# Grouping a scan's small products and moving rotary work to VectorE in an encoder trunk on one Trainium2 core

## The chip, the cores and the metric

The kernel runs on one core of one Trainium2 chip. A core has TensorE (PE in the rows; its weight loads are PEld), VectorE (DVE), ScalarE (ACT), GpSimd (POOL) and SyncE (SP), each with a program of its own that it works off in order, and semaphores between them. The metric is the device time of one execution in microseconds; less is better. The time of a kernel is the median of its runs.

## The reference

The kernel computes a trunk of two post-norm layers on one sequence of 512 tokens, width 1024. Each layer has three groups of heads (differential attention with partial rotary embedding, a bidirectional gated linear recurrence, cross-attention into 256 memory tokens), one output projection, a layer norm, a gated MLP of width 2816 with a width-3 convolution, and a layer norm. Everything is float32. Cut to what matters here:

```python
def hybrid_layer(x, mem, cos, sin, layer, w_in, ...):
    da_q, da_k, da_v, hg_q, hg_ff, hg_fb, hg_i, hg_g, mx_q = jnp.split(x @ w_in, split_idx, axis=-1)
    dq = rope_partial(da_q.reshape(B, S, DA_HEADS, 2, DA_HEAD_DIM), cos, sin) * (DA_HEAD_DIM ** -0.5)
    dk = rope_partial(da_k.reshape(B, S, DA_HEADS, 2, DA_HEAD_DIM), cos, sin)
    ...                                   # differential softmax attention -> da_o
    o_fwd = hgrn2_chunk_scan(hq, -jnp.expm1(g_f), hv, g_f)
    o_bwd = jnp.flip(hgrn2_chunk_scan(...reversed in time...), 1)
    ...                                   # gate and norm -> hg_o; memory attention -> mx_o
    mix = jnp.concatenate([da_o, hg_o, mx_o], axis=-1) @ w_out
    x = layer_norm(DEEPNORM_ALPHA * x + mix, ln1_g, ln1_b)
    u = depthwise_conv_centred(x @ w_up, conv_w, conv_b)
    gate, val = jnp.split(u, 2, axis=-1)
    return layer_norm(DEEPNORM_ALPHA * x + (jax.nn.silu(gate) * val) @ w_down, ln2_g, ln2_b)

def rope_partial(t, cos, sin):            # the first 16 of 64 columns are rotated
    t1, t2 = t[..., :half], t[..., half:ROPE_DIM]
    return jnp.concatenate([t1 * cos - t2 * sin, t2 * cos + t1 * sin, t[..., ROPE_DIM:]], axis=-1)
```

## The kernel before, in words

**Products.** Every large float32 product is made of three float16 products: each operand is split into a high and a low part, and high·high, high·low and low·high are added in PSUM. A weight is read, scaled by a power of two from its sum of squares, and split by `prep`: ScalarE makes the high part, VectorE the low part (L311, `wl`). The same is done for activations (`xh` and `xl`; behind a layer norm, ScalarE at L292 and VectorE at L293 from transposed tiles `tr`) and for the input of the out projection (`mgh`, `mgl`; L545, L547).

**The scan.** Two heads form a unit, two units a layer, so there are four scans. `hg_attn` computes the recurrence by doubling block lengths m = 1, 2, 4 to 256: at each level TensorE makes small products of blocks of both directions for each of the two heads, ScalarE (for small blocks also VectorE at L851 and GpSimd at L854) puts them into a matrix, and VectorE multiplies the decays of a level into Q (L881, on a tile called `t` in the rows), into K (L885) and into the table of decays (L888). The products of the low levels have 32 output partitions, those of m = 64 have 64, the last ones 128. In the rows these are `sc<-t,w 128*32`, `sc<-t,t 128*64` and so on; large products are 128*128. Differential attention contracts over 64 rows (64*128).

**Rotary.** `rope_step` makes a tile of the q or k projection: TensorE's 24 products of 512 columns, then VectorE shuffles the columns (L1003), GpSimd multiplies by the sine (L1004), VectorE multiplies by the cosine (L1005) and adds (L1006), ScalarE rounds to the high part (L1008) and GpSimd subtracts for the low part (L1009). There are 16 such tiles.

**Out projection and LN1.** The out projection is done in parts as groups of heads finish (`down_part`): a product group into a PSUM bank `mm`, which VectorE then adds to the residual `z` (L569). There are two banks for `mm`, three for `sc`, two for `tr` and one for `stat`. When a token tile of `z` is complete, it is normalised (L227 to L232, then L280 and L281 on VectorE, in halves of 512 columns), transposed on TensorE (L288), and split into `xh` and `xl` for the up-projection. LN1 is this layer norm, once in each layer.

**The order.** The program is recorded once, through generators that take turns by credits (a `yield` with a number gives up a turn of that cost; `HG_COST` is 1.6 in the scan). A planner then orders each engine's instructions: it takes the recorded operations with costs (`cost_of`) and the buffers that they hold, simulates the engines, and picks on each engine, among the operations that are ready, the one with the earliest due time. On ScalarE a change of the function table is charged. TensorE's 64-row products take their buffers in runs of six. Which instruction stands where on an engine is thus an outcome of the plan, not of the code's order.

Of the kernel before, what the change touches and what calls it, by code (L numbers as in the profile page):

```python
# [95 lines left out]
def trunk(ctx: ExitStack, tc: tile.TileContext, a, out, slots=None):  # L96
# [595 lines left out]
    def build_layer(l):  # L692
# [55 lines left out]
        def hg_units(pr):  # L748
# [57 lines left out]
            def hg_attn():  # L806
                mix = new_mix(("hg", pr))
                Qs, Ks, As, Ds, Ts = [], [], [], [], []
                for j in range(2):
                    f, q = hs["f", j], hs["q", j]  # L810
                    Q = tmp([P, 2, 512], "t4", bufs=4)
                    K = tmp([P, 2, 512], "t4", bufs=4)
                    V.tensor_tensor(Q, f, q.unsqueeze(1).broadcast_to([P, 2, 512]), ALU.mult)
                    for d in range(2):
                        V.tensor_scalar(K[:, d, :], f[:, 1 - d, :], -1.0, 1.0, ALU.mult, ALU.add)
                    ks = tmp([P, 512], "w2", bufs=4)
                    V.tensor_tensor(ks, K[:, 0, :], K[:, 1, :], ALU.add)
                    At = tmp([P, 4, 512], "t8", bufs=2)
                    Dg = tmp([P, 4, 32], "hgD", bufs=2)
                    p_ = psc()  # L820
                    for c in range(4):
                        for b in range(4):
                            cs = slice(c * P + 32 * b, c * P + 32 * b + 32)
                            mm(p_[32 * b : 32 * b + 32, c * 32 : c * 32 + 32], ks[:, cs], q[:, cs], True, True)
                    A.activation(Dg, p_[:, 0:P].rearrange("p (c t) -> p c t", c=4), AF.Identity)
                    Qs.append(Q)
                    Ks.append(K)
                    As.append(At)
                    Ds.append(Dg)
                    Ts.append(f)  # L830
                    yield HG_COST

                def diag_block(At, s0, t0, n):
                    v = At[s0 : s0 + n, 0, :]
# [3 lines left out]
                while m < S:  # L838
                    nb = S // m
                    for j in range(2):  # L840
# [37 lines left out]
                        if m < 256:  # L878
# [7 lines left out]
                            if m < 128:  # L886
                                Tn = tmp([P, 2, nb // 2], f"hgT{j}_{m.bit_length() % 2}")
                                V.tensor_tensor(Tn, tv[:, :, :, 0], tv[:, :, :, 1], ALU.mult)  # L888
                                Ts[j] = Tn
                        yield HG_COST  # L890
                    m *= 2
                while ("g", 1) not in hs or "v" not in hs:
                    yield None
# [99 lines left out]
        def da_units(pr):  # L993
            ds_ = {}

            def rope_step(ws, key):
                iv = inv_of(ws[0], qin[:, l : l + 1], 0.125 if key == "q" else 1.0)
                ds_["i" + key] = iv
                for j in range(2):
                    p_ = pmm()  # L1000
                    gemm_f(p_, ws[0], j * P, xact)
                    q = tmp([P, 512], "sg", bufs=2)
                    V.stream_shuffle(q, p_, SHUF)  # L1003
                    G.tensor_tensor(q, q, ropes, ALU.mult)  # L1004
                    V.tensor_tensor(p_, p_, ropec, ALU.mult)  # L1005
                    V.tensor_tensor(q, q, p_, ALU.add)  # L1006
                    hl = tmp([P, 2, 512], "qg", F16, bufs=NQG)
                    A.activation(hl[:, 0, :], q, AF.Identity)  # L1008
                    G.tensor_tensor(hl[:, 1, :], q, hl[:, 0, :], ALU.subtract)  # L1009
                    ds_[key, j] = hl  # L1010
                    yield
                if key == "k":
                    ds_["iqk"] = small(1, "iqk", bufs=2)
                    V.tensor_tensor(ds_["iqk"], ds_["iq"], ds_["ik"], ALU.mult)
# [207 lines left out]


class Op:
    __slots__ = ("i", "name", "eng", "cost", "tail", "reads", "writes", "table", "preds", "succs", "tiles", "dmab", "line", "kind", "small", "order_ins", "mv", "istr", "half")


def cost_of(i, kind, eng, outs, ins):
# [56 lines left out]
def extract(instrs):  # L1285
    ops = []
    last_half = None
    for i in instrs:
# [32 lines left out]
        if o.eng == "PE":  # L1321
            if "float16" in str(ins[0].dtype) and ins[0].ap[0][1] == 64:
                o.half = ins[0].offset // ins[0].ap[0][0]
                if last_half not in (None, o.half):
                    o.cost, last_half = 0.005, None
                else:
                    last_half = o.half
            else:
                last_half = None
        ops.append(o)  # L1330

    cache = {}
# [28 lines left out]
    for o in ops:  # L1361
# [16 lines left out]
        for wr, bs in ((False, o.reads), (True, o.writes)):  # L1378
            for b in bs:
# [6 lines left out]
                    else:  # L1386
                        h[:] = [e for e in h if not (p0 <= e[2] and e[3] <= p1 and (e[4] & ~m) == 0 and e[0] != o.i)]
                h.append((o.i, wr, p0, p1, m))
    for o in ops:
        for p in o.preds:  # L1390
            ops[p].succs.append(o.i)
    for o in [o for o in ops if o.dmab][:FIRST]:
        o.dmab *= FAST
    run = []
    for o in ops + [None]:
        if o is not None and o.eng != "PE":
            continue
        if o is not None and o.half is not None:
            run.append(o)
            continue  # L1400
        for k in range(0, len(run), 6):
            both = list(dict.fromkeys(t for p in run[k : k + 6] for t in p.tiles))
            for p in run[k : k + 6]:
                p.tiles = both
        run = []
    return ops, tiles


def simulate(ops, tiles, prio, fixed=None, wait=0.0, log=None):
# [5 lines left out]
    end = [0.0] * N  # L1415
    free = {e: 0.0 for e in ("PE", "DVE", "ACT", "POOL", "SP")}
    table = 0
    dma_free = 0.0

    users = defaultdict(list)  # L1420
# [54 lines left out]
    while done < N:  # L1475
# [24 lines left out]
        if i is None:  # L1500
            a = avail[e]
            lim = t + wait
            i = min((x for x in a if ready[x] <= t + 1e-9), key=lambda x: (prio[x] + (PEN if e == "ACT" and ops[x].table and ops[x].table != table else 0), x))
            if wait:
                w = min((x for x in a if ready[x] <= lim), key=lambda x: prio[x])
                if prio[w] < prio[i]:
# [11 lines left out]
        if e == "ACT" and o.table and o.table != table:  # L1518
            c += 1.28
            table = o.table  # L1520
        start[i] = t
        if o.dmab:
            free[e] = t + o.cost
# [28 lines left out]

PEN = 20.0
SHARE = 0.35
FIRST = 9
FAST = 205 / 370.0

# [88 lines left out]
```

## Time and profile before

| | us |
|---|---|
| median of 3 runs (1499.23 to 1501.7) | 1501.5 |
| profiled execution | 1502.42 |
| its span | 1500.6 |
| TensorE busy | 1457.2 (97%) |
| VectorE busy | 1153.8 (77%) |
| ScalarE busy | 864.2 (58%) |
| GpSimd busy | 167.6 (11%) |

The span is what lies between the first and the last instruction of the profiled execution; the execution's own time is 1.8 us longer. Start times and durations in the rows are counted from the span's start. Busy time on TensorE is modelled, and consecutive products overlap, so that the distance of two starts, not the busy time of one, says what a product costs in a stream.

### The profile page before, as it was taken

Reading aid. Unit: us, or ns where it says so; the run is one execution under the profiler, and the core shown is the slowest. Engines: PE = TensorE matmul, PEld = TensorE weight load, DVE = VectorE, ACT = ScalarE, POOL = GpSimd, SP = SyncE. Lnnn points to the kernel's source line nnn. Section 1 sums busy time; section 2 is a strip of 40 time slices with the busy share of each in tenths; the row PEclk is TensorE's granted clock in tenths of the full one; section 3 lists DMA queues with packets and bytes.
Section 4 is the critical chain, followed back from the end, with each engine's and each line's share of the span. In section 5 each row is a group of like instructions: output and inputs, shape, how many; then the busy total and the mean of one; then the engine's idle time right before and its main releaser. Section 6 shows DMA issues by size and latency. Waiting matters only on the chain. (4 is left out here: it accounts for less than half of the span.)

```text
span 1500.6 us, 24551 instructions
## 1 busy us (share of the span) xinstructions
PE 1457.2 (97%) x9978; PEld 813.0 (54%) x9978; DVE 1153.8 (77%) x2210; ACT 864.2 (58%) x1094; POOL 167.6 (11%) x186
## 2 busy tenths in 40 slices
PE   6999999999999999999999999999999999999997
PEld 4566675555474444444477575655556544444443
DVE  7989967967897667676785969777888777666777
ACT  6876565665376556555456655665644665455550
POOL 1000003030111101001010101122101101001011
PEclk9999999999999999999999999999999999999999
DMA  6342212222143233332334202121232323233221
GB/s 237 113 149 70 74 57 84 88 71 86 43 141 113 85 113 96 101 113 85 113 113 141 84 32 73 70 80 35 84 112 85 112 86 112 95 102 113 85 85 56
DMA packets 158171, 141.91 MB, mean 95 GB/s; under 512 B 3302, under 2 KB 139114, under 8 KB 158058
## 3 DMA queue, kind: packets, MB, share of 16 engines
q1 hardware_dynamic: 158058, 140.35, 29.0%
q8 instruction: 78, 1.28, 0.3%
q14 instruction: 35, 0.29, 0.1%
HBM read 138.24 MB, written 2.10 MB: 94 GB/s over the span
## 5 line engine op out<-in xcount | busy, mean ns | idle before, releaser
L140 PEld LDWEIGHTS <-wh 128*128 128x128 f16 x2624 | 250.5, 98 | 237.6 <-issue 5.1
L311 DVE SCALAR_TENSOR_TENSOR wl<-wst,ws,wh 128x2048 f16<-128x2048 f32 x122 | 312.1, 2558 | 48.4 <-ACT wh L310 47.9
L140 PE MATMUL mm<-xh,wh 128*128 128x512 f16 (+1 forms) x832 | 305.1, 367 | 0.9 <-ACT sg L721 0.8
L140 PE MATMUL mm<-xl,wh 128*128 128x512 f16 (+1 forms) x832 | 305.1, 367 | 0.0
L140 PE MATMUL mm<-xh,wl 128*128 128x512 f16 (+1 forms) x832 | 305.0, 367 | 0.0
L307 ACT ACTIVATE wh<-wst 128x2048 bf16<-128x2048 f32 x122 | 232.3, 1904 | 112.4 <-PE stat L168 44.4
L310 ACT ACTIVATE wh<-wst,ws 128x2048 f16<-128x2048 f32 x122 | 243.5, 1996 | 47.7 <-DVE wi L159 27.6
L140 PE MATMUL mm<-wh,t 128*128 128x512 f16 (+1 forms) x768 | 223.2, 370 | 0.1
L140 PEld LDWEIGHTS <-wl 128*128 128x128 f16 x1312 | 128.2, 98 | 124.4 <-issue 0.6
L140 PEld LDWEIGHTS <-t 128*128 128x128 f16 x1152 | 110.4, 98 | 121.5 <-issue 0.3
L569 DVE SCALAR_TENSOR_TENSOR z<-mm,inv,z 128x512 f32<-128x512 f32 x176 | 130.0, 746 | 48.9 <-PE mm L140 37.5
L140 PE MATMUL sc<-xh,wh 128*128 128x512 f16 (+1 forms) x416 | 147.5, 355 | 1.6 <-ACT xh L292 1.6
L140 PE MATMUL sc<-xh,wl 128*128 128x512 f16 (+1 forms) x416 | 147.4, 354 | 0.0
L140 PE MATMUL sc<-xl,wh 128*128 128x512 f16 (+1 forms) x416 | 147.4, 354 | 0.0
L140 PE MATMUL mm<-wl,t 128*128 128x512 f16 (+1 forms) x384 | 142.1, 370 | 0.0
L1151 POOL TENSOR_TENSOR t<-f 128x512 f32<-128x512 f32 x44 | 56.0, 1272 | 547.0 <-DVE f L1149 426.7
L155 DVE TENSOR_SCALAR we<-stat 128x1 int32<-128x1 int32 x122 | 18.7, 153 | 124.1 <-PE stat L168 123.8
L140 PE MATMUL mm<-wh,mgh 128*128 128x512 f16 x192 | 74.9, 390 | 7.2 <-DVE z L569 7.0
L1147 ACT ACTIVATE f<-sc,cvb,cw 128x512 f32<-128x512 f32 x44 | 34.1, 775 | 72.9 <-PE stat L168 69.0
L140 PE MATMUL mm<-wl,mgh 128*128 128x512 f16 x192 | 75.2, 392 | 0.0
L140 PE MATMUL mm<-wh,mgl 128*128 128x512 f16 x192 | 75.0, 390 | 0.0
L1042 ACT ACTIVATE f<-sc,dam,iqk 128x512 f32<-128x512 f32 x64 | 49.3, 774 | 30.8 <-DVE dam L1040 30.8
(244 smaller groups left out, 2148.8 us busy)
## 6 DMA issues: line engine op xcount, KB each, us to landing
wst<-in_w_up_dram SPq DMA_DIRECT2D x88, 512.0 KB, 4.8
wst<-in_w_in_dram SPq DMA_DIRECT2D x36, 1024.0 KB, 4.8
wst<-in_w_down_dram SPq DMA_DIRECT2D x22, 1024.0 KB, 4.9
wst<-in_w_out_dram SPq DMA_DIRECT2D x12, 1024.0 KB, 4.9
wst<-in_w_mem_kv_dram SPq DMA_DIRECT2D x8, 1024.0 KB, 5.0
z<-in_x_dram SPq DMA_DIRECT2D x4, 512.0 KB, 4.9
mix<-in_ln_g_dram SPq DMA_DIRECT2D x4, 512.0 KB, 5.3
mix<-in_ln_b_dram SPq DMA_DIRECT2D x4, 512.0 KB, 5.0
```

The source lines that it names most:

```text
L140: T.matmul(o, lhsT, rhs, start=start, stop=stop)
L155: V.tensor_scalar(e, tot.bitcast(I32), 0x7F000000, 1, ALU.bitwise_and, ALU.logical_shift_right)
L307: A.activation(h.rearrange("p a b -> p (a b)").bitcast(BF16), flat, AF.Square, accum_out=ss)
L310: A.activation(h.rearrange("p a b -> p (a b)"), flat, AF.Identity, scale=s)
L311: V.scalar_tensor_tensor(l.rearrange("p a b -> p (a b)"), flat, s, h.rearrange("p a b -> p (a b)"), ALU.mult, ALU.subtract)
L569: V.scalar_tensor_tensor(zs, p_, ivs[half % len(ivs)], zs, ALU.mult, ALU.add)
L1042: A.activation(pe[:, c, :], sc_[c], AF.Exp, bias=mx[:, c : c + 1], scale=iqk, accum_out=z1 if c else z0)
L1147: A.activation(c, p_, AF.Identity, scale=cw[:, 1, v : v + 1], bias=cvb[:, l, i + 22 * v : i + 22 * v + 1])
L1151: G.tensor_tensor(gt[:, n, :], c2[:, 0, :], c2[:, 1, :], ALU.mult)
```

## The change

Three things are changed. The scan records both heads' products of a level before it gives up its turn, with the credit of two. In `rope_step` the sine product and the low part are VectorE's. The planner knows a kind for each of TensorE's operations (output partitions 32, 64 or 128, and 0 for differential attention's 64-row products); consecutive operations of one kind other than 128 that hold at most two PSUM tiles form a group in place of the runs of six: each member waits for all inputs of the group and takes all its tiles. In the simulation an operation of another kind than the last has 4.0 added to its due time when the next is picked, and costs 0.093 us more.

```diff
@@ hg_attn
                     Ts.append(f)
-                    yield HG_COST
+                yield 2 * HG_COST
...
                                 Ts[j] = Tn
-                        yield HG_COST
+                    yield 2 * HG_COST
                     m *= 2
@@ rope_step
                     V.stream_shuffle(q, p_, SHUF)
-                    G.tensor_tensor(q, q, ropes, ALU.mult)
+                    V.tensor_tensor(q, q, ropes, ALU.mult)
                     V.tensor_tensor(p_, p_, ropec, ALU.mult)
                     V.tensor_tensor(q, q, p_, ALU.add)
                     hl = tmp([P, 2, 512], "qg", F16, bufs=NQG)
                     A.activation(hl[:, 0, :], q, AF.Identity)
-                    G.tensor_tensor(hl[:, 1, :], q, hl[:, 0, :], ALU.subtract)
+                    V.tensor_tensor(hl[:, 1, :], q, hl[:, 0, :], ALU.subtract)
@@ extract
+        o.mode = 128
+        if o.eng == "PE" and not o.istr:
+            o.mode = 0 if o.half is not None else outs[0].ap[0][1]
         ops.append(o)
...
-    run = []
-    for o in ops + [None]:
-        if o is not None and o.eng != "PE":
-            continue
-        if o is not None and o.half is not None:
-            run.append(o)
-            continue
-        for k in range(0, len(run), 6):
-            both = list(dict.fromkeys(t for p in run[k : k + 6] for t in p.tiles))
-            for p in run[k : k + 6]:
-                p.tiles = both
-        run = []
+    gang, of = [], []
+    for o in [o for o in ops if o.eng == "PE"] + [None]:
+        small = o is not None and o.mode != 128
+        new = small and [t for t in o.tiles if t not in of and "PSUM" in str(tiles[t].space)]
+        if gang and (not small or o.mode != gang[-1].mode or len(held) + len(new) > 2):
+            inside = {g.i for g in gang}
+            ext = set().union(*[g.preds for g in gang]) - inside
+            for g in gang:
+                g.preds |= ext
+                g.tiles = list(dict.fromkeys(g.tiles + of))
+            gang, of = [], []
+        if small:
+            if not gang:
+                held = []
+            gang.append(o)
+            held = list(dict.fromkeys(held + [t for t in o.tiles if "PSUM" in str(tiles[t].space)]))
+            of = held
+    for o in ops:
+        for q in o.preds:
+            ops[q].succs.append(o.i)
     return ops, tiles
@@ simulate
-            i = min((x for x in a if ready[x] <= t + 1e-9), key=lambda x: (prio[x] + (PEN if e == "ACT" and ops[x].table and ops[x].table != table else 0), x))
+            turn = lambda x: PEN if e == "ACT" and ops[x].table and ops[x].table != table else TURN if e == "PE" and ops[x].mode != mode else 0
+            i = min((x for x in a if ready[x] <= t + 1e-9), key=lambda x: (prio[x] + turn(x), x))
...
+        if e == "PE" and o.mode != mode:
+            c += 0.093
+            mode = o.mode
+TURN = 4.0
```

In the listings below a row is one instruction: its line, its operation, output<-inputs with the number of the buffer's use, the output's shape, and how many like it follow one another.

First place: TensorE in the first scan, at the second and third level; `sc_1143` and `sc_1193` are the first head's products, `sc_1168` and `sc_1218` the second head's. Before:

```order
L140 MATMUL sc_1143<-t_168_972,w_196_1144 32x32
L168 LDWEIGHTS ones
L168 MATMUL stat<-wss_1079,ones 128x1
L140 MATMUL sc_1143<-t_168_972,w_196_1144 32x32 x15
L140 MATMUL sc_1168<-t_174_999,w_199_1169 32x32 x16
L140 LDWEIGHTS wh_906
L140 MATMUL mm_1235<-xh,wh_906 128x512
...
L140 MATMUL mm_1235<-xh,wh_906 128x512
L140 MATMUL sc_1193<-t_168_972,w_202_1194 32x32 x16
```

With the change:

```order
L140 MATMUL mm_1260<-xl,wh_906 128x512
L140 MATMUL sc_1143<-t_168_972,w_196_1144 32x32 x16
L140 MATMUL sc_1168<-t_174_999,w_199_1169 32x32 x16
L140 LDWEIGHTS wl_916
L140 MATMUL mm_1260<-xh,wl_916 128x512
...
L140 MATMUL mm_1339<-xl,wh_906 128x512
L140 MATMUL sc_1193<-t_168_972,w_202_1194 32x32 x16
L140 MATMUL sc_1218<-t_174_999,w_205_1219 32x32 x16
```

Before, the two heads' second level stands together but is cut by a `stat` product, and the first head's third level stands alone between two products of a projection. With the change both levels stand in groups of both heads, and the projection runs on for longer between them.

Second place: VectorE at LN1 of layer 0; `z_77` and `z_78` are the first two token tiles, `z_79` is the third, to which the out projection is still being added. Before:

```order
L280 SCALAR_TENSOR_TENSOR z_78<-z_78,bnmv_4570,mix_4488 128x512
...
L280 SCALAR_TENSOR_TENSOR z_78<-z_78,bnmv_4570,mix_4488 128x512
L281 SCALAR_TENSOR_TENSOR z_78<-z_78,lnrs_4572,mix_4492 128x512
L293 SCALAR_TENSOR_TENSOR xl<-tr_4535,lnsc,xh 128x4x128
L293 SCALAR_TENSOR_TENSOR xl<-tr_4544,lnsc,xh 128x4x128
L281 SCALAR_TENSOR_TENSOR z_78<-z_78,lnrs_4572,mix_4492 128x512
L569 SCALAR_TENSOR_TENSOR z_79<-mm_4593,inv_4411,z_79 128x512
L569 SCALAR_TENSOR_TENSOR z_79<-mm_4607,inv_4413,z_79 128x512
L293 SCALAR_TENSOR_TENSOR xl<-tr_4577,lnsc,xh 128x4x128
```

With the change:

```order
L569 SCALAR_TENSOR_TENSOR z_79<-mm_4593,inv_4411,z_79 128x512
...
L280 SCALAR_TENSOR_TENSOR z_77<-z_77,bnmv_4528,mix_4488 128x512
...
L569 SCALAR_TENSOR_TENSOR z_79<-mm_4607,inv_4413,z_79 128x512
...
L281 SCALAR_TENSOR_TENSOR z_78<-z_78,lnrs_4572,mix_4492 128x512
L569 SCALAR_TENSOR_TENSOR z_79<-mm_4621,inv_4507,z_79 128x512
L293 SCALAR_TENSOR_TENSOR xl<-tr_4535,lnsc,xh 128x4x128
L569 SCALAR_TENSOR_TENSOR z_79<-mm_4629,inv_4507,z_79 128x512
L281 SCALAR_TENSOR_TENSOR z_77<-z_77,lnrs_4530,mix_4492 128x512
...
L293 SCALAR_TENSOR_TENSOR xl<-tr_4577,lnsc,xh 128x4x128
...
L293 SCALAR_TENSOR_TENSOR xl<-tr_4544,lnsc,xh 128x4x128
```

The additions of three product groups of `z_79` (L569) have moved ahead of the first L293, and the normalisation of `z_77`'s second half behind them.

Third place: TensorE at LN1 of layer 0, with the transposes `tr` of the normalised tiles, the products `mm` of the out projection and `sc_4766` of the up-projection. Before:

```order
L140 MATMUL mm_4607<-wl_4311,mgh_3024 128x512
L288 MATMUL tr_4535<-cst,z_77 128x128 x4
...
L140 MATMUL mm_4607<-wh_4301,mgl_3039 128x512
L288 MATMUL tr_4544<-cst,z_77 128x128 x4
...
L140 MATMUL mm_4607<-wh_4301,mgl_3042 128x512
L288 MATMUL tr_4577<-cst,z_78 128x128 x4
...
L140 MATMUL sc_4766<-xh,wh_4398 128x256
L288 MATMUL tr_4586<-cst,z_78 128x128 x4
...
L140 MATMUL mm_4621<-wh_4382,mgh_4262 128x512
```

With the change:

```order
L140 MATMUL mm_4607<-wh_4301,mgh_3024 128x512
L288 MATMUL tr_4535<-cst,z_77 128x128 x4
...
L140 MATMUL mm_4607<-wh_4301,mgl_3042 128x512
...
L140 MATMUL mm_4621<-wh_4382,mgh_4262 128x512
...
L140 MATMUL mm_4629<-wh_4382,mgh_4262 128x512
...
L140 MATMUL mm_4663<-wh_4079,mgh_3024 128x512
...
L288 MATMUL tr_4577<-cst,z_78 128x128 x4
...
L140 MATMUL mm_4663<-wh_4079,mgh_3026 128x512
L288 MATMUL tr_4544<-cst,z_77 128x128 x4
```

The transposes of `z_77` and `z_78` stood close together, the last two behind the end of a product group; now they stand one by one among three further product groups, and the first product of the up-projection comes later.

## Rows read from the trace of the kernel before

**Rows 1.** The page, part 1: each engine's busy us (share of the span), instructions.

```profile
PE 1457.2 (97%) x9978; PEld 813.0 (54%) x9978; DVE 1153.8 (77%) x2210; ACT 864.2 (58%) x1094; POOL 167.6 (11%) x186
```

**Rows 2.** TensorE's waits: us in total, times, longest us.

```profile
PE tr L262 <- DVE z L258: 8.9, 4, 4.8
PE mm L140 <- DVE z L569: 7.0, 6, 1.5
PE tr L288 <- DVE xl L293: 3.9, 2, 1.9
...
PE sc L140 <- DVE t L881: 1.9, 3, 0.8
```

**Rows 3.** TensorE in time order, first scan: start us, busy us, what xcount [wait].

```profile
82.38 0.75 PE L140 MATMUL sc<-qg,w 128*32 128x32 f32 x63
82.94 0.22 PE L140 MATMUL sc<-t,w 128*32 128x32 f32 x1
...
95.90 0.38 PE L140 MATMUL mm<-xl,wh 128*128 128x512 f16 x1
96.12 0.38 PE L140 MATMUL mm<-xh,wl 128*128 128x512 f16 x1
96.43 0.76 PE L140 MATMUL sc<-t,w 128*32 128x32 f32 x64
97.12 0.39 PE L140 MATMUL mm<-xh,wh 128*128 128x512 f16 x1
```

**Rows 4.** TensorE in time order, LN1 of layer 0.

```profile
391.82 0.60 PE L288 MATMUL tr<-cst,z 128*128 128x128 f32 x4
392.26 0.38 PE L140 MATMUL mm<-wh,mgl 128*128 128x512 f16 x1
...
393.99 0.38 PE L140 MATMUL mm<-wh,mgl 128*128 128x512 f16 x1
396.30 0.72 PE L288 MATMUL tr<-cst,z 128*128 128x128 f32 x4 [1.93 <-DVE xl L293]
...
398.82 0.63 PE L140 MATMUL mm<-wh,mgh 128*128 128x512 f16 x1
...
403.77 0.27 PE L140 MATMUL sc<-xl,wh 128*128 128x256 f16 x1
```

**Rows 5.** Windows: us, busy of PE, PEld, DVE, ACT, POOL, PEclk, DMA share, GB/s.

```profile
398.80:403.80 5.00, 5.00 (x15) 1.78 (x13) 2.98 (x6) 0.69 (x1) 0.00 (x0) 0.52 0.00 2
```

**Rows 6.** VectorE in time order, LN1 of layer 0.

```profile
395.51 1.40 DVE L293 SCALAR_TENSOR_TENSOR xl<-tr,lnsc,xh 128x512 f16<-128x512 f32 x2
396.83 0.74 DVE L281 SCALAR_TENSOR_TENSOR z<-z,lnrs,mix 128x512 f32<-128x512 f32 x1
397.49 0.74 DVE L569 SCALAR_TENSOR_TENSOR z<-mm,inv,z 128x512 f32<-128x512 f32 x1
```

**Rows 7.** TensorE in time order, LN1 of layer 1.

```profile
1133.71 0.38 PE L140 MATMUL mm<-wh,mgh 128*128 128x512 f16 x1
...
1137.99 0.27 PE L140 MATMUL sc<-xl,wh 128*128 128x256 f16 x1
```

**Rows 8.** VectorE in time order, first scan.

```profile
95.44 2.34 DVE L311 SCALAR_TENSOR_TENSOR wl<-wst,ws,wh 128x2048 f16<-128x2048 f32 x1
97.70 1.29 DVE L881 TENSOR_TENSOR t<-t,hgT 128x512 f32<-128x512 f32 x2
98.90 0.30 DVE L851 COPY_PREDICATED hgD<-masks,sc 128x128 f32<-128x128 uint8 x1
...
100.03 0.42 DVE L885 TENSOR_TENSOR t<-t,hgT 128x256 f32<-128x256 f32 x1
100.36 0.15 DVE L157 TENSOR_SCALAR ws<-we 128x1 int32<-128x1 int32 x1
```

**Rows 9.** VectorE's groups by line: xcount | busy us, mean ns | idle before <-releaser.

```profile
L1006 DVE TENSOR_TENSOR sg<-sg,mm 128x512 f32<-128x512 f32 x16 | 11.0, 687 | 4.0 <-POOL sg L1004 4.0
```

**Rows 10.** Windows, the rotary tiles of layer 0 (columns as in group 5).

```profile
230.00:256.00 26.00, 26.00 (x148) 15.20 (x147) 19.23 (x49) 14.47 (x28) 8.69 (x7) 1.00 0.25 82
```

More of the change, by code (lines that the diff above doesn't have):

```diff
@@ L1224 @@
 class Op:
-    __slots__ = ("i", "name", "eng", "cost", "tail", "reads", "writes", "table", "preds", "succs", "tiles", "dmab", "line", "kind", "small", "order_ins", "mv", "istr", "half")
+    __slots__ = ("i", "name", "eng", "cost", "tail", "reads", "writes", "table", "preds", "succs", "tiles", "dmab", "line", "kind", "small", "order_ins", "mv", "istr", "half", "mode")
 def cost_of(i, kind, eng, outs, ins):
@@ L1388, in extract @@
                 h.append((o.i, wr, p0, p1, m))
-    for o in ops:
-        for p in o.preds:
-            ops[p].succs.append(o.i)
     for o in [o for o in ops if o.dmab][:FIRST]:
         o.dmab *= FAST
-    run = []
-    for o in ops + [None]:
-        if o is not None and o.eng != "PE":
-            continue
-        if o is not None and o.half is not None:
-            run.append(o)
-            continue
-        for k in range(0, len(run), 6):
-            both = list(dict.fromkeys(t for p in run[k : k + 6] for t in p.tiles))
-            for p in run[k : k + 6]:
-                p.tiles = both
-        run = []
+    gang, of = [], []
[18 more added lines that the diff above has]
+            ops[q].succs.append(o.i)
     return ops, tiles
@@ L1417, in simulate @@
     table = 0
+    mode = 128
     dma_free = 0.0
```

## The prediction

> **What bounds the kernel now.** I read the engines' totals first [rows 1]: TensorE is busy 1457.2 of 1500.6 us, VectorE 1153.8, GpSimd 167.6. TensorE is the bound, and only two things can shorten the kernel: fewer or shorter intervals on TensorE, or less of its 43.4 us (1500.6 − 1457.2) of idle time. Second, TensorE's waits [rows 2]: the largest, 8.9 us for L258, belongs to the input's layer norm at the start, in which the orders before and after are the same. What the change can touch are the 7.0 us for VectorE's evictions of the out projection (L569, 6 waits), 3.9 us for xl of the layer norm (L293, 2 waits) and 1.9 us for the scan's product on VectorE (L881, 3 waits). Third, two stretches in time order: the scan, where small products cut into the stream of projections [rows 3], and LN1, the layer norm behind the out projection [rows 4 to 7].
>
> **Changes of tile kind.** TensorE's program has 175 places where a product with 32 or 64 output partitions, or with 64 contracted rows (differential attention), stands next to one of another kind; with the change it has 145, 30 fewer, nearly all in the four scans: 128 to 32 falls from 37 to 29, 32 to 128 from 33 to 29, 128 to 64 from 8 to 4, 64 to 128 from 12 to 4, 32 to 64 from 4 to 0. The price is in start-to-start times. A 512-column product starts 0.22 us behind its neighbour (95.90, 96.12), but 0.31 pass before the first small product (96.12 to 96.43): 0.09 for going in. The 64 small ones then take 0.69 until the next large one (96.43 to 97.12), where 63 of them without a change took 0.56 (82.38 to 82.94), so 64 take 0.57: 0.12 for coming out [rows 3]. Thirty times that is between 2.8 and 3.6 us. I take 0.093 for all but those four or so pairs whose exit is dearer: **−3.1 us**. No wait hides it, because TensorE is the engine that everything waits for.
>
> Beside that price stands a rule. The Trainium skill, "TensorEngine Tiling (Array Packing)", section Tiling Modes, says that a change of the tiling mode drains TensorE. By it the change would be worth what is left of the product in flight, which is rival 1 below; by the rows it is worth 2.8 to 3.6.
>
> **LN1 of layer 0.** Before, the last product of the out projection's group starts at 393.99, the next instruction at 396.30, 2.31 us later where 0.22 is usual: 2.09 lost. From there to 398.82 are 2.52 us for eight transposes and one 256-column product, which take 0.99 (four transposes 0.44, from 391.82 to 392.26; half of 0.22): 1.53 lost. Then 12 products take 4.95 us (398.82 to 403.77) in place of 12 × 0.216 = 2.59: 2.36 lost [rows 4]; in that stretch the granted clock is 0.52, so about the lower of TensorE's two levels, 1.2 GHz, after TensorE had lost 3.6 of 4.8 us [rows 5]. Together 6.0 us. The cause stands on VectorE: at 395.51 two L293, then L281, and only at 397.49 the L569 that gives back a bank of the two "mm" banks in PSUM, without which no further out product may start [rows 6]. In the changed order VectorE has the evictions L569 of mm_4593, mm_4607 and mm_4621 ahead of the first L293, and TensorE has the four groups of transposes spread over three product groups. I walked this by hand from T, the start of the products into mm_4509, with 0.216 for a product, 0.74 for an L569 or L281, 0.70 for an L293 [rows 6]: the banks come free at T + 8.9, 11.7 and 13.1, and TensorE wants them at T + 10.8 (four groups of 6 products, two of 12, four transposes), 12.1 and 13.4. None is late, so the clock has no reason to fall either. What is late next: the low part of the last gate block is computed later (L547), about 0.55 at mm_4509, and the second half of tile 1 (tr_4586) stands behind a weight split on VectorE, about 0.6 at the up-projection. Left 1.15, so 6.0 − 1.15: **−4.8 us**. Bounds: 0 (the wait only moves) and −6.0 (nothing left).
>
> **LN1 of layer 1.** Here 12 products take 4.28 (1133.71 to 1137.99) for 2.59, 1.69 lost [rows 7]; with its wait of 1.9 [rows 2] and 1.2 around it, 4.8 in all. The order stays nearly as it was: two L281 still stand ahead of the eviction that frees the bank. My walk leaves 2.4 of waiting and 1.7 of low clock: **−0.7 us**, bounds +2 and −4.8.
>
> **The scan's groups.** A group of small products now starts when both heads' inputs are there, and TensorE, which runs in order, holds everything behind it until then. From the second level's pair (sc_1143, sc_1168) to the pair of the 64-wide level, TensorE's own work in the changed order is 24.1 us. VectorE has to issue in the same stretch ten L881 at 0.60 (two from 97.70 to 98.90), sixteen L885 at 0.33 (100.03 to 100.36), three weight splits L311 at 2.26 (95.44 to 97.70) [rows 8] and some 35 smaller ones, together about 7.0: 6.0 + 5.3 + 6.8 + 7.0 = 25.1, so 25.1 − 24.1 = 1.0 us of waiting in the first scan. Before, VectorE was already never idle here, and its work was the same; what TensorE gained was that one head could go on while the other was late. For each of the other three scans I take what one wait for L881 has cost so far, 1.9 / 3 = 0.6 [rows 2], 1.8 together. Sum **+2.8 us**, bounds 0 and +10 (four scans at 2.5, one split ahead of the group).
>
> **Down parts between.** The order of L569 at the six waits of 7.0 us [rows 2] changes by single places; walking them gives 2.05 for 1.85 at the first, and for the others 5.5 for 6.9, the low clock behind them included. These walks are no better than 2 us each: **0**, bounds −3 and +3.
>
> **Rotary.** Thirty-two operations go to VectorE, 16 sine products and 16 low parts. A neighbour of the same shape, L1006, takes 687 ns and waited 4.0 us in all for the sine product from GpSimd [rows 9]. VectorE gets 32 × 0.69 = 22 us more, less those 4.0 of waiting. In the rotary stretch VectorE is busy 19.2 of 26 us [rows 10] and takes about 3.5 per rotary tile, under the 5.2 us that TensorE needs for its 24 products. The cover is that gap: **0**. If it were gone, the 18 us net would fall on TensorE in part; half the tiles late by one operation is 8 × 0.69 = 5.5, the upper bound. Nothing on TensorE waits now for L1009, so there is no gain to have.
>
> **Sum.** −3.1 − 4.8 − 0.7 + 2.8 + 0 + 0 = −5.8. The profiled execution took 1502.4 us, 1.8 more than its span and 0.9 above the median of 1501.5, inside the runs' 1499.2 to 1501.7 but for 0.7. 1502.4 − 5.8 = 1496.6, and for the median 1495.7.
>
> **The rivals.** (1) *A change of kind costs the drain.* If each change cost what is left of a product when the next could start, 0.38 − 0.22 = 0.16 by the busy time and distance of the large product [rows 3], 30 of them are 4.9, and the time is 1501.5 − 4.9 − 4.8 − 0.7 + 2.8 = 1493.9. Against it: the rows show 0.09 and 0.12. (2) *LN1's stall stays.* The planner's order rests on its own costs; if L280 and L281 run late, the transposes wait as before in another place, and −3.1 + 2.8 leaves 1501.2. For it: VectorE has the same operations for LN1 as before and only 0.3 us of slack at the walk's tightest bank (13.1 for 13.4). Against it: three evictions moved ahead. (3) *The groups wait* and the kernel is slower. If each of the 28 groups waits 0.63, the row for L881, that is 17.6 in place of 2.8: 1495.7 + 14.8 = 1510.5. It decides from (8.6 + 3.0) / 28 = 0.41 us a group, 8.6 being the other gains and 3.0 being 0.2%. For it: VectorE is never idle in the scan. Against it: three of some forty groups waited so far.
>
> **How the numbers follow.** About 0.2%, 3 us, is what a measurement of this kernel tells from no change. Forecast 0.58, its own range 1492.5 to 1499.5 (the gain at LN1 and the scan's price each off by 2 to 3 us); drain 0.08; stall stays 0.22; groups wait 0.12. Faster than 1498.5: 0.53 of the forecast and 0.08 of the drain, 0.61. Within 3 us: the forecast's upper end 0.05, the stall 0.22, a mild form of waiting groups 0.02, together 0.29. Slower: 0.10. The range reaches down to the drain with the LN1 bound, 1491.5, and up over the stall that stays with the down parts' bound, 1503.5; above it lie the waiting groups.
>
> **What would show it.** Right: the LN1 rows of layer 0 with no wait over 1 us for L293 and no stretch of granted clock near half behind them; 29 places of 128 to 32 with 0.31 ahead of each; waits for L881 of 2 to 5 us in total; VectorE at about 1153.8 + 22 us; no TensorE wait for L1004, L1009 or a rotary eviction. Wrong: L881, or the copies behind it, above 10 us among TensorE's waits; a wait for L569 or L293 at LN1 of 2 us or more with the slow clock behind it; new waits at rotary tiles.

## The result, and the profile after

The changed kernel takes 1492.62 us (median of 4 runs, 1492.08 to 1493.01), the kernel before 1501.05 on the same chip: ratio 0.9939, 95% interval 0.9926 to 0.9951. The forecast was 1495.7 in 1491.5 to 1503.5, so the sign and the range held and the gain, 8.4 us, was larger than the 5.8 forecast. The ratios compare fast executions alone; one of the kernel with only the planner's part, 1897.5 us at a mean granted clock of 0.754, is left out of them. The profiled execution has a span of 1491.1 us (1500.6 before); before, it took 1.4 us more than the median, and after 0.3 more, so that the two spans differ by 9.5. The page's first part, beside [rows 1]:

```profile
PE 1451.7 (97%) x9978; PEld 811.9 (54%) x9978; DVE 1168.4 (78%) x2242; ACT 865.1 (58%) x1094; POOL 130.1 (9%) x154
```

TensorE has 5.5 us less of busy time and 39.4 us of idle time in place of 43.4. VectorE has 14.6 us more of busy time. The 32 operations' durations add up to 22.0 us, those of all others to 2.7 less than before, and the page counts time in which two operations overlap once. The 4.0 us for which L1006 waited for GpSimd [rows 9] are gone too, but that was idle time and is no part of the 14.6.

```profile
L1009 DVE TENSOR_TENSOR qg<-sg,qg 128x512 f16<-128x512 f32 x16 | 11.0, 687 | 2.8 <-ACT qg L1008 2.7
L1004 DVE TENSOR_TENSOR sg<-sg,ropes 128x512 f32<-128x512 f32 x16 | 11.0, 687 | 0.0
...
L1006 DVE TENSOR_TENSOR sg<-sg,mm 128x512 f32<-128x512 f32 x16 | 10.9, 683 | 0.0
```

TensorE's waits (us in total, times, longest), beside [rows 2]:

```profile
PE mm L140 <- DVE z L569: 4.7, 6, 2.7
...
PE tr L513 <- DVE f L1051: 2.1, 2, 1.3
PE sc L140 <- DVE hgD L851: 1.9, 5, 0.4
PE sc L140 <- DVE t L881: 1.5, 4, 0.5
...
PE mm L140 <- DVE wl L311: 0.6, 1, 0.6
PE mm L140 <- DVE mgl L547: 0.6, 1, 0.6
```

The two waits of 1.9 us for L293 are gone, those for L569 are 2.3 us less, and the scan now also waits for L851, the copy on VectorE. The 2.1 us for L1051 are new; they lie in the attention and down parts of layer 0.

To see where the time went, both orders of TensorE were cut at places where the same products lie behind in both. For each stretch the table has the difference in length, and how much of it the distances give: each pair of neighbours at the median start-to-start distance that such a pair has in the trace of before, summed along each order (this is where changes of kind count). The rest is idle time, low clock, and distances that differ from their median. Sorting the pairs by shape alone moves a row of the distances by 0.4 us at most.

| stretch of before, us | length before, after | difference | by distances | rest |
|---|---|---|---|---|
| start, 4 to 31 | 27.0, 28.0 | +1.0 | 0 | +1.0 |
| scans of layer 0, 82 to 201 | 119.1, 118.2 | −0.9 | −1.6 | +0.7 |
| rotary tiles, 230 to 268 | 38.0, 38.1 | +0.2 | 0 | +0.2 |
| attention and down parts, 268 to 360 | 91.8, 88.9 | −2.8 | −0.4 | −2.4 |
| out projection, 360 to 389 | 29.3, 30.1 | +0.8 | 0 | +0.8 |
| LN1 of layer 0, 389 to 423 | 33.9, 28.1 | −5.8 | −0.2 | −5.6 |
| MLP, 423 to 836 | 412.9, 412.6 | −0.3 | +0.2 | −0.5 |
| scans of layer 1, 836 to 930 | 93.7, 95.7 | +2.1 | −1.4 | +3.5 |
| attention and down parts of layer 1, 994 to 1107 | 113.1, 109.5 | −3.6 | −1.1 | −2.5 |
| LN1 of layer 1, 1123 to 1140 | 17.1, 16.8 | −0.3 | 0 | −0.3 |

With 0.1 in what is left out, that is −9.5, the difference of the two spans.

LN1 of layer 0 in the changed kernel, TensorE in time order, beside [rows 4]:

```profile
381.68 0.39 PE L140 MATMUL mm<-wh,mgl 128*128 128x512 f16 x1 [0.57 <-DVE mgl L547]
...
389.89 0.60 PE L288 MATMUL tr<-cst,z 128*128 128x128 f32 x4
390.33 0.38 PE L140 MATMUL mm<-wl,mgh 128*128 128x512 f16 x1
...
395.30 0.60 PE L288 MATMUL tr<-cst,z 128*128 128x128 f32 x4
395.73 0.38 PE L140 MATMUL mm<-wh,mgh 128*128 128x512 f16 x1
...
396.60 0.60 PE L288 MATMUL tr<-cst,z 128*128 128x128 f32 x4
397.03 0.38 PE L140 MATMUL mm<-wl,mgh 128*128 128x512 f16 x1
```

No group of transposes waits. The only wait between 376 and 400 us is the 0.57 us for the low part of the gate block, which the prediction's walk had at 0.55. The granted clock in a window over it (columns as in [rows 5]) is 1.00, the upper of the two levels:

```profile
389.00:400.00 11.00, 11.00 (x58) 5.81 (x57) 10.71 (x22) 3.75 (x4) 1.78 (x2) 1.00 0.01 2
```

And VectorE there, beside [rows 6]:

```profile
389.48 0.75 DVE L569 SCALAR_TENSOR_TENSOR z<-mm,inv,z 128x512 f32<-128x512 f32 x1
...
392.26 0.75 DVE L569 SCALAR_TENSOR_TENSOR z<-mm,inv,z 128x512 f32<-128x512 f32 x1 [0.28 <-PE mm L140]
...
393.65 0.74 DVE L569 SCALAR_TENSOR_TENSOR z<-mm,inv,z 128x512 f32<-128x512 f32 x1
394.31 0.74 DVE L293 SCALAR_TENSOR_TENSOR xl<-tr,lnsc,xh 128x512 f16<-128x512 f32 x1
394.97 0.74 DVE L569 SCALAR_TENSOR_TENSOR z<-mm,inv,z 128x512 f32<-128x512 f32 x1
```

Three evictions L569, at 389.48, 392.26 and 393.65, now stand before the first L293 at 394.31. The second waits for TensorE: VectorE is early, and the bank is back in time.

The scan of layer 0, one pair of heads on TensorE:

```profile
96.72 0.38 PE L140 MATMUL mm<-xl,wh 128*128 128x512 f16 x1
97.15 0.46 PE L140 MATMUL sc<-t,w 128*32 128x32 f32 x32
97.96 0.46 PE L140 MATMUL sc<-t,w 128*32 128x32 f32 x32 [0.35 <-DVE hgD L851]
98.35 0.39 PE L140 MATMUL mm<-xh,wl 128*128 128x512 f16 x1
```

Both heads' 32 records stand side by side with a projection's products around them, and the second head is not ready: 0.35 us for VectorE's L851.

### The profile page after: what moved, and what is told of

Read it like the earlier page. It is cut to its first block, busy times and chain, and to the rows that moved or that the text cites. A ratio compares the mean times of both kernels' runs of the same rounds, so it can differ in the third digit from the quotient of the medians.

```text
span 1491.1 us, 24496 instructions
## 1 busy us (share of the span) xinstructions
PE 1451.7 (97%) x9978; PEld 811.9 (54%) x9978; DVE 1168.4 (78%) x2242; ACT 865.1 (58%) x1094; POOL 130.1 (9%) x154
## 5 line engine op out<-in xcount | busy, mean ns | idle before, releaser
L311 DVE SCALAR_TENSOR_TENSOR wl<-wst,ws,wh 128x2048 f16<-128x2048 f32 x122 | 312.5, 2561 | 52.3 <-ACT wh L310 51.4
L569 DVE SCALAR_TENSOR_TENSOR z<-mm,inv,z 128x512 f32<-128x512 f32 x176 | 130.2, 745 | 45.9 <-PE mm L140 32.2
L1151 POOL TENSOR_TENSOR t<-f 128x512 f32<-128x512 f32 x44 | 60.6, 1378 | 542.7 <-DVE f L1149 438.6
```

The source lines that it names most:

```text
L311: V.scalar_tensor_tensor(l.rearrange("p a b -> p (a b)"), flat, s, h.rearrange("p a b -> p (a b)"), ALU.mult, ALU.subtract)
L569: V.scalar_tensor_tensor(zs, p_, ivs[half % len(ivs)], zs, ALU.mult, ALU.add)
L1151: G.tensor_tensor(gt[:, n, :], c2[:, 0, :], c2[:, 1, :], ALU.mult)
```

## The experiments

All times are medians, the ratio is to the kernel before on the same chip in the same session (1501.1 to 1501.8 there), with its 95% interval; it need not be the quotient of two medians shown here. "Changes" are changes of tile kind in TensorE's program; the few transposes of 16 to 44 rows (L242, L406, L470) are counted too.

**The parts apart.** The change has three: the recording (both heads of a level before the turn is given up), the planner's part (kinds, groups, turn cost, charge), and rotary on VectorE. Each run takes some of the edits shown in the front part and leaves the others as before.

| recording | planner | rotary | changes | us | ratio |
|---|---|---|---|---|---|
| new | | | 167 | 1498.23 | 0.9986 [0.9975, 0.9998] |
| | new | | 161 | 1499.49 | 0.9980 [0.9971, 0.9988] |
| | | new | 171 | 1504.81 | 1.0019 [1.0011, 1.0028] |
| new | new | | 149 | 1496.42 | 0.9965 [0.9953, 0.9977] |
| | new | new | 157 | 1493.80 | 0.9943 [0.9930, 0.9955] |
| new | new | new | 145 | 1492.62 | 0.9939 [0.9926, 0.9951] |

*Recording alone*:

```diff
-                        yield HG_COST
+                    yield 2 * HG_COST
```

> Only the recording of the scan: both heads of a level before the turn is given up, planner and rotary as before. TensorE's program has 167 changes of tile kind (175 before, 145 with the whole change) and the order at LN1 of layer 0 is that of before. Theory (the planner's new order at LN1 and between the parts of the out projection brings most, fewer changes of kind the rest): 8 changes fewer are 0.8 us, paid for by waits of one head for the other; 1501 us, between 1499.5 and 1503, with the 6.0 us at LN1 still there. Rival (the two heads' grouping is what brings the gain): 1494 to 1496.

1498.23, between the two theories. Its profile has the scans 1.2 us shorter, the down parts of layer 1 1.1 shorter, and LN1 of both layers 2.8 shorter, at the same order in layer 0 and nearly the same in layer 1: there the waits are as before and the low clock behind them lasted less. That part is not the edit's: low clock comes and goes between profiles of one order (last section).

*Planner alone*: the edits in `extract` and `simulate`, `TURN = 4.0`.

> Only the planner's part: kinds, groups, the turn cost and the charge; recording and rotary as before. 161 changes of kind; VectorE's order at LN1 of layer 0 is that of the whole change. Theory: 14 changes fewer are 1.5 to 2 us, LN1 of layer 0 gives 5 to 6, so 1493.5 to 1495. Rival (grouping by the recording brings the gain, the planner only carries it): above 1498.

1499.49: the theory was too hopeful, and the time is where the rival had it. In its profile LN1 of layer 0 is 5.8 us shorter, as in the whole change. But the scans are 3.1 us longer although the distances give 1.8 less, so 4.9 of rest, and the rotary tiles of layer 0 are 1.0 longer. My theory had no term for that. The profiled execution, at 1496.81, is 2.7 us faster than the median, so these stretches do not account for all of the 1499.49.

*Rotary alone*:

```diff
-                    G.tensor_tensor(q, q, ropes, ALU.mult)
+                    V.tensor_tensor(q, q, ropes, ALU.mult)
-                    G.tensor_tensor(hl[:, 1, :], q, hl[:, 0, :], ALU.subtract)
+                    V.tensor_tensor(hl[:, 1, :], q, hl[:, 0, :], ALU.subtract)
```

> Only the rotary part on VectorE; recording and planner as before. 171 changes of kind, order at LN1 as before. Theory: nothing on TensorE waits for rotary, 0 to -1 us, 1500 to 1501.5. Rival (the 4.0 us that VectorE waited for the sine product come back on TensorE): 1497.

1504.81, slower than either theory. The rotary tiles of layer 0 are as long as before. The 125 us from them to LN1 are 3.2 us longer: TensorE has 1.8 us more of idle time there, and the granted clock is 0.97 for 0.99. Nothing there is a rotary operation: the planner, with other costs, found another order.

*Recording and planner, without rotary*.

> The whole change without its rotary part. 149 changes of kind. Theory: as the whole change, 1492.6, up to 1 us above it. Rival (rotary brings 4 us): 1496 to 1497.

1496.42. Beside the planner alone the scans are 2.2 us shorter in the two profiles. But 3.8 us are missing to the whole change, as the rival had it, and for a reason that it did not name (below).

*Planner and rotary, without the recording*.

> The whole change without its recording: planner and rotary. 157 changes of kind against 145. Theory (recording saves the 12 changes, 1.2 to 1.4 us, and some of the waits in the scans): 1494 to 1496. Rival (rotary brings nothing of its own beside the planner): the time of the planner alone, 1499.5, less what this run shares with the whole change by chance.

1493.80, 1.2 us above the whole change with 12 changes more and 0.2 under the theory's range; the rival fell. The two intervals overlap almost wholly (0.9930 to 0.9955, and 0.9926 to 0.9951), so beside the planner and rotary the recording, which was to group the scan's products, has no gain that these runs can tell.

**The price of a change of kind.** Into the kernel before go 80 extra products in the MLP's up-projection (`gemm_f`, ahead of the fifth of eight steps), where TensorE never waits; their results are not read:

```diff
+            if extra and k == 4:
+                pt = ptr()
+                mm(pt[0:32, 0:32], ident[:, 0:32], ident[:, 0:32], True, True)
```

> The kernel before with 80 extra products of 32 output partitions (identity columns into an unread PSUM tile), one in the middle of each of 80 groups of 24 products of the MLP's up-projection, where TensorE never waits: 160 more changes of tile kind, nothing else. Theory (0.09 in and 0.12 out): 80 x 0.21 = 17 us, and some 1 us for the products themselves, 1518 to 1520. Rival (a change costs the drain, 0.16 each): 26 us, 1527. Rival (changes cost nothing in a dense stream): 1502.

and as a control `mm(pt[:, 0:32], ident, ident[:, 0:32], True, True)`:

> The control: the same 80 extra products with 128 output partitions, so no change of kind. Only their own columns: four passes of 32 columns at 2.4 GHz are 0.05 us, 80 of them 4 us: 1505 to 1506. If the extra cost in the run with 32 partitions were that of any foreign small product, this one would cost the same 17 us.

1524.65 (ratio 1.0154 [1.0138, 1.0170]) and 1513.53 (1.0076 [1.0058, 1.0095]): 22.8 us / 80 = 0.285 and 11.7 / 80 = 0.146. Both are above the expectation of my theory. TensorE in time order around one insertion, first with 32 output partitions, then the control:

```profile
435.75 0.38 PE L140 MATMUL mm<-xh,wl 128*128 128x512 f16 x1
436.06 0.25 PE L140 MATMUL tr<-cst 128*32 128x32 f32 x2
436.24 0.39 PE L140 MATMUL mm<-xh,wh 128*128 128x512 f16 x1
```

```profile
435.62 0.38 PE L140 MATMUL mm<-xh,wl 128*128 128x512 f16 x1
435.83 0.30 PE L140 MATMUL tr<-cst 128*128 128x32 f32 x2
435.97 0.38 PE L140 MATMUL mm<-xh,wh 128*128 128x512 f16 x1
```

Going in is 0.31 for 0.22, as in [rows 3]; the small product and the way out take 0.18. The control's two records take 0.14 with no change of kind. These are the medians of all 80 places too: 0.309 and 0.181, and 0.216 and 0.140 in the control, so the way in costs 0.093 and in the control nothing. So a pair of changes costs between 0.285 − 0.146 = 0.139 (if the small product itself cost what the control's does) and 0.285 less the 0.01 to 0.02 that one such product takes in a row of them, that is 0.07 to 0.13 for a change. The drain as I had priced it, 0.16 a change and thus 0.32 a pair beside the product, is excluded as a mean. The Trainium skill, "TensorEngine Tiling (Array Packing)", section Tiling Modes, says that a change of mode drains TensorE; these rows agree that it costs time, and give it no more than 0.13 on average.

**LN1's evictions.** The changed kernel, with VectorE's order edited after planning: the last three L569 ahead of the first L293, and the one after it, go behind the next L281. All other engines' orders are the changed kernel's.

```diff
+    dv = order["DVE"]
+    at = lambda line, k: next(j for j in range(k, len(dv)) if ops[dv[j]].line == line)
+    f = at(293, 0)
+    late = [j for j in range(f) if ops[dv[j]].line == 569][-3:] + [at(569, f)]
+    n = at(281, f) + 1
+    order["DVE"] = [i for j, i in enumerate(dv[:n]) if j not in late] + [dv[j] for j in late] + dv[n:]
```

> The whole change, with VectorE's order altered at one place: at LN1 of layer 0 the four evictions L569 of z_79 (mm_4593, mm_4607, mm_4621, mm_4629) are moved behind the first L293 and the L281 after it, 3 to 13 rows later, as they stood before the change. TensorE's order and all else is that of the changed kernel. Theory (these evictions give back the mm banks): by the rows of the changed kernel the eviction of mm_4593 ends at 393.9 in place of 390.2, TensorE wants the bank at 392.1, so it waits 2.0 us, and with a fall of the clock behind it up to 4.4: 1494.5 to 1497. Rival (the wait at LN1 went away for another reason, the transposes' new places): 1492.6, no new wait.

1497.42 (ratio 0.9965 [0.9953, 0.9978]), 4.8 us above the changed kernel and 0.4 above the theory's range. TensorE at the place:

```profile
392.83 0.38 PE L140 MATMUL mm<-wh,mgl 128*128 128x512 f16 x1
395.50 0.59 PE L140 MATMUL mm<-wh,mgh 128*128 128x512 f16 x1 [2.30 <-DVE z L569]
395.88 0.63 PE L140 MATMUL mm<-wl,mgh 128*128 128x512 f16 x1
396.31 0.63 PE L140 MATMUL mm<-wh,mgl 128*128 128x512 f16 x1
```

The wait is 2.30 us, and the products behind it stand 0.43 apart; the granted clock from 395.5 to 398.9 is 0.50, the lower level. LN1 took 4.1 us more in this profile. TensorE's 9978 records stand in the same order in both kernels, and nowhere but here does the late one fall more than 1 us further behind. So it is shown that LN1's gain, with the transposes where they are, needs these four evictions in their place.

**Rotary: the engine or the order.** Two kernels hold the order and change the engine. In the first the planner takes the 32 operations for VectorE's, and they are put into GpSimd's order by their planned start; in the second the other way round.

```diff
         o.line = i.debug.lineno if i.debug else 0
+        if o.line in (1004, 1009):
+            o.eng = "DVE"
...
+    rot = [i for i in order["DVE"] if ops[i].line in (1004, 1009)]
+    order["DVE"] = [i for i in order["DVE"] if i not in rot]
+    order["POOL"] = sorted(order["POOL"] + rot, key=lambda i: start[i])
```

> The changed kernel's order on TensorE, ScalarE, SyncE and on VectorE for all that stays there, but the 32 rotary operations are executed by GpSimd: planned as VectorE's, then put into GpSimd's order by their planned start. Theory (what rotary brought beside the planner's part, 1496.4 to 1492.6, is another order of the work behind it, not the engine): 1492.5 to 1494. Rival (VectorE's faster operation itself is the gain): about 1496.4.

> The other corner: the order of the run without the rotary part, with the 32 operations executed by VectorE at their planned start. Theory (the order): 1496 to 1497. Rival (the engine): 1492.6.

| order planned for | executed by VectorE | executed by GpSimd |
|---|---|---|
| VectorE | 1492.62, 0.9939 [0.9926, 0.9951] | 1492.87, 0.9947 [0.9935, 0.9960] |
| GpSimd | 1501.95, 1.0002 [0.9993, 1.0011] | 1496.42, 0.9965 [0.9953, 0.9977] |

In each row TensorE's 9978 records stand in the same order. At the better order the engine makes no difference that can be told. At the other order VectorE makes it slower. The expectations of both theories for that run, 1496 to 1497 and 1492.6, were missed: over layer 0's rotary tiles its TensorE has 1.3 us of idle time against 0.4 with the same order on GpSimd, and between 973 and 1060 us, in layer 1's rotary and attention, it falls 2.5 us further behind, in steps of 0.3 to 0.7. That fits operations which, put into VectorE's queue at places planned for another engine, delay what stands behind them; which of them do wasn't traced. The two windows, first on GpSimd, then on VectorE (columns as in [rows 5]; length less PE's busy time is the idle time):

```profile
229.55:268.58 39.03, 38.59 (x243) 22.74 (x241) 28.23 (x66) 23.48 (x44) 11.74 (x7) 1.00 0.23 75
```

```profile
229.55:269.96 40.41, 39.09 (x243) 22.81 (x241) 31.41 (x74) 24.05 (x44) 0.00 (x0) 1.00 0.21 72
```

So the 3.8 us of rotary are the planner's order. In the profiles they lie in layer 1's attention and down parts: windows over the same two pieces of work, first before, then recording and planner, then the whole change, then its order with GpSimd (columns as in [rows 5]):

```profile
994.00:1031.15 37.15, 35.31 (x228) 19.75 (x226) 33.33 (x69) 25.90 (x46) 4.48 (x3) 1.00 0.25 86
1065.12:1107.10 41.98, 38.91 (x238) 21.99 (x236) 37.50 (x81) 29.05 (x51) 2.41 (x4) 1.00 0.27 86
```

```profile
988.29:1025.33 37.04, 35.43 (x228) 19.45 (x226) 33.28 (x69) 24.41 (x43) 3.95 (x3) 1.00 0.26 86
1059.44:1103.33 43.89, 40.96 (x240) 22.37 (x238) 37.76 (x81) 29.28 (x51) 2.41 (x4) 0.96 0.21 71
```

```profile
988.30:1023.71 35.41, 34.62 (x229) 19.72 (x226) 31.17 (x67) 23.75 (x41) 2.09 (x2) 1.00 0.26 87
1057.72:1097.81 40.09, 38.65 (x239) 22.22 (x238) 38.06 (x83) 29.24 (x51) 1.21 (x2) 1.00 0.27 89
```

```profile
989.26:1024.67 35.41, 34.62 (x229) 19.70 (x226) 31.16 (x66) 23.82 (x41) 2.69 (x3) 1.00 0.24 87
1058.69:1098.77 40.08, 38.65 (x239) 22.21 (x237) 38.06 (x83) 29.26 (x51) 1.21 (x2) 1.00 0.25 90
```

Length less TensorE's busy time is 1.8 + 3.1 = 4.9 us before, 1.6 + 2.9 = 4.5 without rotary, and 0.8 + 1.4 = 2.2 in both last ones. In the second piece of the second kernel the clock is 0.96 too. The two pieces are 5.4 us shorter in the whole change than without rotary, more than the 3.8 of the medians: the profiled execution without rotary took 1498.70, 2.3 above its median, and the ten of that kernel range from 1493.48 to 1500.15.

**Turn cost and groups.** `TURN = 8.0` in place of 4.0:

> The whole change with the turn cost at 8.0 in place of 4.0: 135 changes of tile kind in place of 145. By 0.14 us a change, which the runs with extra products bound, 10 fewer are 1.4 us: 1491 if nothing else moves. If small products held back longer make TensorE wait for the next level: 1493 to 1496.

1503.66 (1.0020 [1.0011, 1.0029]), above both expectations. The changes fell to 135 and the distances give 2.3 us less than with 4.0, but TensorE has 12 us more of waiting and low clock, most of it at layer 1's first scan and at the down parts.

And the whole change with the runs of six in place of the groups:

> The whole change without the groups (members no longer wait for one another's inputs, runs of six as before), the turn cost kept: 143 changes of kind, and at LN1 of layer 0 VectorE has two evictions and not four among the first L293. Theory (groups cost waits in the scans, 4 us more than before in the whole change, but bring LN1's order): scans 2 to 4 us shorter, LN1 2 to 5 us longer, 1491 to 1496. Rival (the groups are what saves the changes of kind): 4 us and more slower than the whole change.

1499.41 (0.9991 [0.9982, 0.9999]), 6.8 us above the whole change. LN1 of layer 0 is 3.0 us longer, as expected. The scans are not shorter: they are 2.8 us longer than before, where the whole change has 1.2, at about the same distances. And from layer 0's rotary tiles to LN1 it takes 3.3 us more than the whole change, which neither theory had. My theory that members waiting for one another cost the scans 4 us falls. The rival's time came true, its reason did not, since there are two changes of kind fewer than with the groups. Waits that come with the planner's part come without the groups too; the turn cost and the charge for a change, which hold small products back, are what the two have in common, but alone they weren't run, and the cause stays open.

## Why the prediction held, step by step

**Changes of kind, −3.1.** Right in place, too small: −4.5 by the distances, an estimate. (The prediction's own rows, 0.093 for 26 changes and 0.12 for four, give 2.9.) The way in is confirmed: of the 29 places of 128 to 32, those without a wait have 0.309 ahead of them in the median. At the 0.13 that the extra products allow at most, 30 changes are 3.9; what makes up the 4.5 beyond that, other neighbours in the new order among it, wasn't separated.

**LN1 of layer 0, −4.8.** Right: −5.8 in the stretch and +0.8 ahead of it, so −5.0, with the gate block's wait within 0.02. The late evictions show the mechanism. The size was in part luck. The forecast took the 2.4 us of low clock in the one profile of before as the order's own; with rotary alone, where both engines' order at LN1 of layer 0 and the wait of 1.93 are those of before, the clock did not fall and the stretch took 31.4 us (last section). Against that the change gains 3.3 and not 5.8. The 0.6 at the up-projection is there as 0.58, TensorE waiting for the weight split L311 itself and not for the transposed tile behind it.

**LN1 of layer 1, −0.7.** Measured −0.3 in the profiled execution, with a wait of 2.7 for L569 where the walk left 2.4, and the low clock behind it. By its words that is a sign of being wrong (2 us or more for L569 at LN1 with the slow clock), although its own walk of this layer had it. At the same order with rotary on GpSimd the clock did not fall, and the stretch is 2.0 shorter than before.

**The groups in the scan, +2.8.** The size was low: +4.2 of rest (0.7 and 3.5). The granted clock is 1.00 in all four scans; 2.3 of the 4.2 are idle time of TensorE (2.9 us before, 5.2 after), the remainder distances longer than their medians. The waits for L881 are 1.5 us, under the 2 to 5 that were to show it, and 1.9 for L851 stand beside them. The reason was wrong, or at least not the one needed, since without groups it is 6.0.

**Down parts, 0 with bounds −3 and +3.** This is the term that failed: −4.9 of idle time and low clock in the two stretches, outside its bounds. That the order changes by single places was no reason for 0: TensorE's waits for L569 in the two stretches fell from 7.0 to 2.1 us, and in layer 1 these places halved the idle time. (The 2.7 at LN1 of layer 1 make up the 4.7 of the list.) The walk itself came out at −1.2 (2.05 for 1.85, 5.5 for 6.9) and was set to 0 because of its error of 2 us each. Layer 1's part, −2.5, stands in all three profiles with the changed order there. Of layer 0's −2.4, about 1.3 is the clock: the profile of the same order with rotary on GpSimd has a stretch of low clock there at 348 us, and 90.2 us for the 88.9. Without that, −3.6 is left.

**Rotary, 0.** Right for the operations themselves at the order that was planned for VectorE, shown with the order held; at GpSimd's order they cost 5.5 us. But the edit also changed the costs that the planner saw, and through its order it made 3.8 us with the rest of the change, and a loss of 0.2% alone. The prediction had no step for that.

The start took 1.0 us more, at an order that is the same; 0.2 to 1.4 in the other profiles, so that is the execution's. The rivals: the drain's price is excluded, LN1's wait of layer 0 went away, and the groups' wait, 4.2 / 28 = 0.15 us, stayed under the 0.41 us a group from which it would have decided.

That the number held is partly luck: the scans' miss of +1.4 and that of the changes, −1.4, cancel, and what was put at nothing, the down parts, is larger than the miss of the total. The 1492.62 lies at the edge of the forecast's own range, 1492.5 to 1499.5. And the lower end of the whole range, 1491.5, does not follow from its sentence: the drain with the LN1 bound is 1493.9 − 1.2 = 1492.7.

## What to carry to other kernels

When a planner orders the engines, an edit's direct cost and its effect on the order are two terms; hold the order and change the engine, or hold the program and move a few rows, before crediting the edit. A few evictions that give back a PSUM bank are worth more than many cheaper operations, because a wait for one can be followed by a low clock: 2.30 us of waiting made 4.1 here. Edits that each gain little, or lose, can be worth some four times their sum together (here −2.1, −3.0 and +2.9 by the ratios, each give or take 1.3 to 1.8, −9.2 in all), so they are to be timed together too. They are to be taken away one at a time as well: planner and rotary without the recording have −8.6 of the −9.2.

## What the runs showed of the hardware

The same order and the same wait do not always bring the same clock. TensorE at LN1 of layer 1, first in the changed kernel, then in the run without the recording, which has the same wait:

```profile
1123.20 0.58 PE L140 MATMUL mm<-wh,mgh 128*128 128x512 f16 x1 [2.66 <-DVE z L569]
1123.58 0.63 PE L140 MATMUL mm<-wl,mgh 128*128 128x512 f16 x1
1124.01 0.63 PE L140 MATMUL mm<-wh,mgl 128*128 128x512 f16 x1
```

```profile
1125.38 0.38 PE L140 MATMUL mm<-wh,mgh 128*128 128x512 f16 x1 [2.66 <-DVE z L569]
1125.60 0.38 PE L140 MATMUL mm<-wl,mgh 128*128 128x512 f16 x1
1125.81 0.38 PE L140 MATMUL mm<-wh,mgl 128*128 128x512 f16 x1
```

After 2.66 us of waiting the products stand 0.43 apart in the one and 0.22 in the other; the granted clock over the next 3.3 us is 0.50 and 1.00. The same at LN1 of layer 0 with the order of before and its wait of 1.93, in the kernel before, with the recording alone, and with rotary alone (columns as in [rows 5]):

```profile
389.02:422.95 33.93, 31.03 (x187) 19.25 (x186) 30.16 (x54) 13.69 (x15) 5.24 (x7) 0.90 0.14 44
```

```profile
389.31:422.08 32.77, 29.88 (x187) 18.91 (x186) 30.04 (x54) 13.35 (x15) 5.25 (x7) 0.95 0.15 46
```

```profile
393.83:425.28 31.45, 28.23 (x188) 18.24 (x187) 29.87 (x54) 13.70 (x15) 5.23 (x7) 1.00 0.16 50
```

The changed order, with no such wait, takes 28.1 us. A single profile therefore says little about differences under 2.5 us at such a place.

Two float32 records of 32 columns into 128 partitions cost 0.14 us in a stream of 512-column float16 products, more than the 0.05 expected from their columns.
